# A fused transformer kernel: the bonus term, the chunk decay and the halving of tanh in the RWKV pairs are placed elsewhere

## The chip, the cores and the metric

The kernel runs on one core of a Trainium2 chip. Its time is device microseconds, the median of several runs. The engines are called PE (TensorE, the matmuls), PEld (its weight loads), DVE (VectorE), ACT (ScalarE), POOL (GpSimd) and SP (SyncE, here only for transfers).

## The reference

A first block of two layers (mixers, cross attention, convolutional feed-forward) runs over 512 tokens of width 1024 and is not touched. The second block has an RWKV-7 mixer with 8 heads of 64 channels, beside a banded attention. What matters, cut from the reference:

```python
def token_shift(p, mu):
    prev = jnp.pad(p, ((0, 0), (1, 0), (0, 0)))[:, :-1]
    return p + mu * (prev - p)

def rwkv7_step(state, inp):
    r_t, w_t, k_t, v_t, a_t, b_t = inp
    sa = jnp.einsum('bhij,bhj->bhi', state, a_t)
    state = state * w_t[:, :, None, :] + sa[..., None] * b_t[:, :, None, :] + v_t[..., None] * k_t[:, :, None, :]
    y = jnp.einsum('bhij,bhj->bhi', state, r_t)
    return state, y

def rwkv7_mix(ps, w0, w2, a0, a2, k_k, k_a, r_k, lnx_g, lnx_b):
    ...
    w_log = -jax.nn.softplus(-(w0 + jnp.tanh(wd) @ w2).astype(f32)) - 0.5
    decay = jnp.exp(-jnp.exp(w_log))
    a = jax.nn.sigmoid((a0 + ad @ a2).astype(f32))
    ...
    kk = k * k_k.astype(f32).reshape(N_RWKV_HEADS, HEAD_DIM)
    kk = kk / jnp.maximum(jnp.sqrt(jnp.sum(kk * kk, axis=-1, keepdims=True)), 1e-12)
    k = k * (1.0 + (a - 1.0) * k_a.astype(f32).reshape(N_RWKV_HEADS, HEAD_DIM))
    _, y = lax.scan(rwkv7_step, state0, (r, decay, k, v, -kk, kk * a))   # over the tokens
    ...
    bonus = jnp.sum(r * k * r_k.astype(f32), axis=-1, keepdims=True) * v
    y = y + bonus.reshape(b_, s_, D_RWKV)
    return y.astype(ps.dtype), g
```

(`y` is normalised per head between the scan and the bonus.)

## The kernel before

The second block works on transposed data: 128 channels on the partitions, 512 tokens along the free axis. Two heads make one tile, so the RWKV mixer is four pairs, `rwkv_pair(0)` to `rwkv_pair(3)`. Each pair is worked out for eight chunks of 64 tokens at once; then `rwkv_invert` inverts the 64 x 64 triangles of all pairs, through two transfers by way of DRAM, and `rwkv_chain` walks through the eight chunks, with the state of all four pairs in one tile `st`.

All through this stretch, PE is also given linear products of the second block's input projections, each a run of 24 matmuls (8 slices of K, three terms each: L304, L305 and L306) into one PSUM bank of tag "mm". They are the background: `fill(us)` hands out some microseconds' worth of them at places written into `rwkv_pair` (the table `FILL`), `need(...)` hands out as many as a pair needs to have its r, k and v. A scheduler then orders the instructions of each engine; the pair's own work has high priority, the matmuls and transposes stay in the order in which the program issues them. PSUM has 2 banks of tag "mm", 2 of "at", 1 of "pv" and 3 of "ch".

An "mm" bank of r, k or v is read by the token shift: an ACT copy `t` (L839), a DVE multiply-add over columns 1 to 511 (L841), and a DVE correction of column 0 alone (L843, 128x1). Only when all have read it can the next linear products use that bank.

The steps of a pair, in the order in which it needs them: the two lora products `pw`, `pa` (tags ch), the square of k (ACT L952), two tanh (ACT L954), each made a sigmoid by a DVE multiply-add (L955), the norm product `pk` against `ones_h`, DVE L959, the reciprocal root (L390 to L394: an ACT table load and activation, ACT square, three DVE instructions), kk (DVE L962), the new k (ACT L964, DVE L965), **the bonus** (DVE L967 makes r * r_k * k, a product `pb` against `ones_h` sums it over each head, DVE L971, ACT L972, a transfer of the result to DRAM, `yd`, by POOL's queue), the running sum of the decay's exponent (DVE scan L977) and its exponentials, the tiles `ar` (L986, L987 POOL) and `bk` (L991 DVE and L992 POOL, half of the partitions each; L988 POOL multiplies kk for it), eight transposes of v with DVE copies into `sav` (L1010 to L1015), the products of `ar` with `bk`, 32 in all, their masks (DVE L1033), a transfer of the triangles for the inversion, the decay of bk to the end of its chunk (DVE L1044, `c<-c,pc`) and its transposes, 16 products of `mk1` with `sav`, each of them for both heads, and the copy of their result to `y` (ACT L1061).

The table's `rt` is the tag of six rotating 128x512 tiles (`sg`, `av`, `q`, `u`, `kk`, `pt`), `c` the tag of bk, `rk` that of r, k and v, `xh` and `w` those of the background's operands.

## Time and profile before

| | |
|---|---|
| runs | 1797.75 us, median of 3 (1796.97 to 1798.38) |
| profiled execution | 1802.54 us, of which the span is 1800.8 us |
| mean granted clock of PE | 0.989 |
| busy | PE 98%, PEld 82%, DVE 60%, ACT 41%, POOL 25% |
| second block's pairs, inversion and chain | about 1425 to 1700 us of the span |

The rows further on come from the profiled execution. Its span is counted from the first to the last instruction; starts are microseconds from the span's begin. A row of the timeline gives start, duration, engine, line, operation and output<-inputs, and in brackets how long the engine idled ahead of it and which instruction ended that. A duration includes time in which the instruction had started and was held up. "PEclk" is the granted clock as a share of full speed.

### The profile page before, as it was taken

What the parts mean: (1) busy time and instruction counts of PE and PEld (TensorE: products, weight loads), DVE (VectorE), ACT (ScalarE), POOL (GpSimd) and SP (SyncE); (2) the same over time, 40 slices, a digit from 0 to 9 for tenths busy, and PEclk for the clock granted to TensorE, in tenths of its full rate; (3) what the DMA queues carried; (4) which work ended last, traced back from release to release, by engine and by line L of the source; (5) the groups of instructions that cost most, each with busy time, mean ns of one, the idle gap of its engine ahead of it and who ended that gap; (6) DMA issues with size and microseconds to landing.
All of it is one profiled execution on the core that took longest, in us unless ns stands there. A gap on an engine that the chain in (4) does not pass through costs nothing.

```text
span 1800.8 us, 25750 instructions
## 1 busy us (share of the span) xinstructions
PE 1761.9 (98%) x10200; PEld 1474.8 (82%) x10200; DVE 1088.5 (60%) x1649; ACT 745.3 (41%) x1231; POOL 443.7 (25%) x500
## 2 busy tenths in 40 slices
PE   8999999999999999999999999999999989999999
PEld 7889989888888888888998988888888866776667
DVE  5675756864653468544565675465455785774672
ACT  5544544532332347332354453233234543434561
POOL 0125115110100042000511543554354142210122
PEclk9999999999999999999999999999999999999999
DMA  8431312653532244432131256676663434461332
GB/s 283 155 106 48 129 36 71 206 181 115 196 99 94 74 125 130 140 94 94 50 127 36 71 193 228 245 275 227 221 226 104 137 123 179 177 199 65 136 124 92
DMA packets 67096, 252.50 MB, mean 140 GB/s; under 512 B 7840, under 2 KB 10528, under 8 KB 59296
## 3 DMA queue, kind: packets, MB, share of 16 engines
q1 hardware_dynamic: 47376, 175.92, 29.7%
q0 software_dynamic: 14768, 66.07, 10.4%
q10 hardware_dynamic: 4832, 8.88, 1.5%
q8 instruction: 80, 1.31, 0.3%
q14 instruction: 40, 0.33, 0.1%
HBM read 212.30 MB, written 38.54 MB: 139 GB/s over the span
## 4 chain that ended last, share of the span: by engine, by line
PE 82%; DVE 10%; ACT 4%; issue 2%; DMA 2%; SPq 0%; ACTq 0%; DVEq 0%
PE ch L305 11%; PE ch L304 11%; PE ch L306 11%; PE mm L304 10%; PE mm L306 10%; PE mm L305 10%; PE pv L305 4%; PE pv L304 3%; PE pv L306 3%; PE ch L907 3%; DVE x L447 1%; DVE xh L451 1%; PE at L1266 1%; DVE w L230 1%; DVE x L446 1%
## 5 line engine op out<-in xcount | busy, mean ns | idle before, releaser
L304 PE MATMUL mm<-xh,w 128*128 128x512 f32 (+1 forms) x680 | 258.2, 380 | 9.8 <-ACT w L229 6.5
L306 PE MATMUL mm<-xh,w 128*128 128x512 f32 (+1 forms) x680 | 252.6, 372 | 0.8 <-DVE w L230 0.8
L305 PE MATMUL mm<-xh,w 128*128 128x512 f32 (+1 forms) x680 | 251.5, 370 | 0.0
L229 ACT CAST w<-raw 128x1024 fp32r<-128x1024 f32 (+2 forms) x98 | 98.7, 1008 | 151.7 <-PE ch L306 62.7
L304 PEld LDWEIGHTS mm<-xh,w 128*128 128x128 f32 x680 | 130.1, 191 | 37.3 <-issue 9.6
L229 ACT CAST wx<-raw 128x1024 fp32r<-128x1024 f32 (+1 forms) x85 | 88.1, 1039 | 160.9 <-PE ch L306 68.9
L305 PE MATMUL ch<-xh,w 128*128 128x512 f32 (+1 forms) x424 | 151.5, 357 | 0.3
L304 PE MATMUL ch<-xh,w 128*128 128x512 f32 (+1 forms) x424 | 150.8, 356 | 1.0 <-ACT xh L450 1.0
L306 PE MATMUL ch<-xh,w 128*128 128x512 f32 (+1 forms) x424 | 150.5, 355 | 0.0
L306 PEld LDWEIGHTS mm<-xh,w 128*128 128x128 f32 x680 | 130.1, 191 | 24.8 <-issue 3.2
L305 PEld LDWEIGHTS mm<-xh,w 128*128 128x128 f32 x680 | 130.3, 192 | 24.4 <-issue 4.6
L230 DVE TENSOR_TENSOR w<-rawx,w 128x1024 fp32r<-128x1024 f32 (+2 forms) x85 | 116.2, 1367 | 52.6 <-ACT w L229 52.2
L230 DVE TENSOR_TENSOR w<-raw,w 128x1024 fp32r<-128x1024 f32 (+2 forms) x90 | 122.9, 1367 | 40.0 <-ACT w L229 39.4
L230 DVE TENSOR_TENSOR wx<-raw,wx 128x1024 fp32r<-128x1024 f32 (+1 forms) x85 | 117.5, 1384 | 26.5 <-ACT wx L229 26.1
L414 POOL TENSOR_TENSOR t<-x,x 128x512 f32<-128x512 f32 x6 | 8.5, 1417 | 498.3 <-DVE x L423 333.0
L229 ACT CAST w<-rawx 128x1024 fp32r<-128x1024 f32 (+2 forms) x85 | 87.3, 1027 | 100.0 <-PE mm L306 57.3
L304 PE MATMUL ch<-xh,wx 128*128 128x512 f32 (+1 forms) x288 | 100.7, 350 | 0.0
L306 PE MATMUL ch<-xh,wx 128*128 128x512 f32 (+1 forms) x288 | 100.2, 348 | 0.0
L305 PE MATMUL ch<-xh,wx 128*128 128x512 f32 (+1 forms) x288 | 100.2, 348 | 0.0
L304 PE MATMUL mm<-hd,w 128*128 128x256 f32 (+1 forms) x292 | 94.7, 325 | 0.0
L306 PE MATMUL mm<-hd,w 128*128 128x256 f32 (+1 forms) x292 | 94.7, 324 | 0.0
L305 PE MATMUL mm<-hd,w 128*128 128x256 f32 (+1 forms) x292 | 94.7, 324 | 0.0
(499 smaller groups left out, 4450.3 us busy)
## 6 DMA issues: line engine op xcount, KB each, us to landing
raw<-in_up SPq DMA_DIRECT2D x56, 512.0 KB, 3.6
sp_in_r<-vt POOLq DMA_DIRECT2D x20, 1024.0 KB, 5.2
w<-sp_in_r SPq DMA_DIRECT2D x20, 1024.0 KB, 5.0
rawx<-in_up SPq DMA_DIRECT2D x32, 512.0 KB, 3.6
kt<-in_ada POOLq DMA_DIRECT2D x24, 512.0 KB, 5.7
raw<-in_dn SPq DMA_DIRECT2D x24, 512.0 KB, 4.2
vt<-in_in_r POOLq DMA_DIRECT2D x20, 512.0 KB, 6.8
raw<-in_c_in SPq DMA_DIRECT2D x16, 512.0 KB, 3.5
```

The source lines that it names most:

```text
L229: nc.scalar.copy(hi, src)
L230: (eng or nc.vector).tensor_tensor(out=lo, in0=src, in1=f32(hi), op=ALU.subtract)
L304: mm(out, lhsT=ah, rhs=bh, start=start, stop=False)
L305: mm(out, lhsT=ah, rhs=bl, start=False, stop=False)
L306: mm(out, lhsT=al, rhs=bh, start=False, stop=stop)
L414: eng.tensor_tensor(out=sz, in0=self.x[0][:, ts] if m == 1 else sz, in1=z, op=ALU.add)
L446: (nc.vector if k in DVE_SUB else nc.gpsimd).tensor_tensor(out=x, in0=x, in1=mn, op=ALU.subtract)
L447: nc.vector.scalar_tensor_tensor(out=x, in0=x, scalar=gk, in1=rs, op0=ALU.mult, op1=ALU.mult)
L451: nc.vector.scalar_tensor_tensor(out=lo, in0=x, scalar=bk, in1=f32(hi), op0=ALU.add, op1=ALU.subtract)
L907: self.tc.keep_in_program_order(self.nc.tensor.matmul(out, **kw))
L1266: nc.tensor.matmul(ps[hs, :w], lhsT=q[hs, c * 64 : c * 64 + 64], rhs=k[hs, :w], start=True, stop=True)
```

## The change

Three edits in the second block:

- The bonus moves from the middle of a pair to its end. r * r_k * k is made behind the masks (L1039 in the new numbering); the product against `ones_h`, the multiply by v (L1061), the activation (L1062) and the transfer stand behind the pair's last products and the copy of `y`.
- The decay to the chunk's end is no longer multiplied into `bk` (L1044 goes), nor into the old state in the middle of a chunk's step; the sum of the old state and the step's products is multiplied once, behind the addition. The first step multiplies what it copied before.
- The sigmoid's `0.5 * tanh + 0.5` is an ACT activation (L958) in place of a DVE instruction.

```diff
--- before.py
+++ after.py
@@ -827,6 +827,8 @@
             nc.vector.tensor_scalar(out=t, in0=self.vec[:, s : s + n], scalar1=0.5, scalar2=None, op0=ALU.mult)
         self.qg = self.const.tile([P, 1], F32, tag="qg", name="qg")
         nc.vector.tensor_scalar(out=self.qg, in0=self.v("q_norm_g_2", 0), scalar1=0.125, scalar2=None, op0=ALU.mult)
+        self.half = self.const.tile([P, 1], F32, tag="half", name="half")
+        nc.vector.memset(self.half, 0.5)
         self.reset = self.pool.tile([P, S], BF16, tag="reset", name="reset")
         nc.vector.memset(self.reset, 1.0)
         nc.vector.memset(self.reset.rearrange("p (c t) -> p c t", c=8)[:, :, 0:1], 0.0)
@@ -942,6 +944,7 @@
         wad = self.got[16]
         self.need(self.got, (j, 4 + j, 8 + j))
         r, k, v = self.got[j], self.got[4 + j], self.got[8 + j]
+        got_v = v
         cs = slice(j * P, j * P + P)
         pa, pw = self.bank("ch"), self.bank("ch")
         self.mm(pw, lhsT=self.lora[0:64, cs], rhs=wad[0:64, :], start=True, stop=True)
@@ -952,7 +955,7 @@
         nc.scalar.activation(q, k, AF.Square, scale=self.v("k_k_2", j))
         for o, ps, b in ((sg, pw, self.hw0), (av, pa, self.ha0)):
             nc.scalar.activation(o, ps, AF.Tanh, bias=b[:, j : j + 1], scale=0.5)
-            nc.vector.tensor_scalar(out=o, in0=o, scalar1=0.5, scalar2=0.5, op0=ALU.mult, op1=ALU.add)
+            nc.scalar.activation(o, o, AF.Identity, bias=self.half, scale=0.5)
         self.fill(FILL[0])
         pk = self.bank("ch")
         self.mm(pk, lhsT=self.c("ones_h"), rhs=q, start=True, stop=True)
@@ -963,14 +966,7 @@
 
         nc.scalar.activation(u, av, AF.Identity, bias=self.ka1[:, j : j + 1], scale=self.v("k_a_2", j))
         nc.vector.tensor_tensor(out=k, in0=k, in1=u, op=ALU.mult)
-
-        nc.vector.scalar_tensor_tensor(out=u, in0=r, scalar=self.v("r_k_2", j), in1=k, op0=ALU.mult, op1=ALU.mult)
         self.fill(FILL[1])
-        pb = self.bank("ch")
-        self.mm(pb, lhsT=self.c("ones_h"), rhs=u, start=True, stop=True)
-        nc.vector.scalar_tensor_tensor(out=u, in0=pb, scalar=64.0, in1=v, op0=ALU.mult, op1=ALU.mult)
-        nc.scalar.activation(u, u, AF.Identity, bias=self.v("lnx_b_2", j))
-        nc.gpsimd.dma_start(out=self.yd[j], in_=u)
 
         e = float(np.exp(-0.5))
         c = q
@@ -1040,8 +1036,9 @@
                                     in_=m1[ob : ob + 32, hh, :, 32 * b : 32 * b + 32])
             nc.scalar.copy(sav[o : o + 32, :, o : o + 32], m1[o : o + 32, hh, :, 32:64])
 
+        nc.vector.scalar_tensor_tensor(out=u, in0=r, scalar=self.v("r_k_2", j), in1=k, op0=ALU.mult, op1=ALU.mult)
+
         bkf = bk.rearrange("p c b t -> p c (b t)")
-        nc.vector.tensor_tensor(out=bkf, in0=bkf, in1=pc.unsqueeze(2).to_broadcast([P, 8, P]), op=ALU.mult)
         bh = self.big("bh").rearrange("p (c t) -> p c t", c=8)
         for c4 in range(2):
             self.fill(FILL[4])
@@ -1059,6 +1056,11 @@
                 o, v = slice(64 * hh, 64 * hh + 64), slice(64 - 64 * hh, 128 - 64 * hh)
                 self.mm(ps[o, cc * 64 : cc * 64 + 64], lhsT=m1[v, hh, cc, :], rhs=sav[v, cc, o], start=True, stop=True)
         nc.scalar.copy(y, ps)
+        pb = self.bank("ch")
+        self.mm(pb, lhsT=self.c("ones_h"), rhs=u, start=True, stop=True)
+        nc.vector.scalar_tensor_tensor(out=u, in0=pb, scalar=64.0, in1=got_v, op0=ALU.mult, op1=ALU.mult)
+        nc.scalar.activation(u, u, AF.Identity, bias=self.v("lnx_b_2", j))
+        nc.gpsimd.dma_start(out=self.yd[j], in_=u)
         return dict(j=j, ar=ar, mk=m2, bh=bh, sav=sav, pc=pc, y=y)
 
     def rwkv_invert(self, prs):
@@ -1146,9 +1148,6 @@
                     for i, pr in enumerate(prs):
                         for o in heads:
                             self.mm(ps[o, col(i)], lhsT=st[o, i, :], rhs=pr["ar"][o, cc, 1, :], start=i == 0, stop=False)
-                    if cc < 7:
-                        nc.vector.tensor_tensor(out=st, in0=st, in1=pc4[:, :, cc : cc + 1].to_broadcast([P, 4, 64]),
-                                                op=ALU.mult)
                     yield
                 for i in range(4):
                     for o in heads:
@@ -1165,10 +1164,12 @@
                         self.mm(ps[o, col(i)], lhsT=sav4[:, i, cc, o], rhs=pr["mk"][:, hh, cc, :], start=False, stop=i == 3)
                 if cc < 7:
                     sn = self.t("st", [P, 256], F32, 2).rearrange("p (i t) -> p i t", i=4)
-                    if cc == 0:
-                        nc.vector.tensor_copy(sn, four(ps[:, 256:]))
-                    else:
-                        nc.vector.tensor_tensor(out=sn, in0=st, in1=four(ps[:, 256:]), op=ALU.add)
+                    got = four(ps[:, 256:])
+                    if cc:
+                        nc.vector.tensor_tensor(out=sn, in0=st, in1=got, op=ALU.add)
+                        got = sn
+                    nc.vector.tensor_tensor(out=sn, in0=got, in1=pc4[:, :, cc : cc + 1].to_broadcast([P, 4, 64]),
+                                            op=ALU.mult)
                     st = sn
                 nc.scalar.copy(rs, four(ps[:, :256]))
                 yield
```

The new line numbers are two or three higher than the old ones down to the bonus's old place (the token shift's L839, L841 and L843 become L841, L843 and L845; the tanh's L954 becomes L957), and three or four lower behind it (bk's L991, L992 and L988 become L987, L988 and L984, the masks' L1033 becomes L1029).

How the order of the engines' instructions moves, at three places. First DVE in pair 1, between the norm's multiplies and the products of `ar` and `bk`; `mm_12312` is the bank of the last-but-one linear output before PE's next two, `sav` the transposed v, `c_1618` or `c_1617` is bk. Before:

```order
L841 SCALAR_TENSOR_TENSOR rk_12371<-mm_12312,mu_12054,t_1620_12372 128x511
L393 TENSOR_SCALAR rt_12304<-rt_12304 128x512
L977 SCALAR_TENSOR_TENSOR rt_12303<-reset,rt_12301 128x512
L394 TENSOR_TENSOR rt_12322<-rt_12322,rt_12304 128x512
L843 TENSOR_SCALAR rk_12371<-mm_12312,mu_12054 128x1
L962 SCALAR_TENSOR_TENSOR rt_12322<-rk_12177,vec,rt_12322 128x512
L994 COPY pc_1563_12076<-rt_12354 128x8
L965 TENSOR_TENSOR rk_12177<-rk_12177,rt_12304 128x512
L986 SCALAR_TENSOR_TENSOR ar_12358<-rt_12322,rt_12301 128x8x64
L967 SCALAR_TENSOR_TENSOR rt_12304<-rk_12097,vec,rk_12177 128x512
L841 SCALAR_TENSOR_TENSOR rk_12420<-mm_12378,mu_12054,t_1627_12421 128x511
L991 TENSOR_TENSOR c_1618_12359<-rt_12322,rt_12303 64x8x64
```

And of the changed kernel, in which L843 of the same bank (`rk_12366<-mm_12313`) stands one row ahead of this piece:

```order
L965 SCALAR_TENSOR_TENSOR rt_12323<-rk_12173,vec,rt_12323 128x512
L1006 COPY sav_1562_12077<-ch_12380 64x4x64
L990 COPY pc_1563_12078<-rt_12349 128x8
L1008 COPY sav_1562_12077<-ch_12380 64x3x64
L1009 COPY sav_1562_12077<-ch_12380 64x64
L968 TENSOR_TENSOR rk_12173<-rk_12173,rt_12305 128x512
L982 SCALAR_TENSOR_TENSOR ar_12353<-rt_12323,rt_12302 128x8x64
L1006 COPY sav_1562_12077<-ch_12398 64x4x64
L1011 COPY sav_1562_12077<-ch_12398 64x4x64
L987 TENSOR_TENSOR c_1617_12354<-rt_12323,rt_12304 64x8x64 x2
L1039 SCALAR_TENSOR_TENSOR rt_12305<-rk_12099,vec,rk_12173 128x512
L845 TENSOR_SCALAR rk_12366<-mm_12313,mu_12054 128x1
```

The 128x1 correction of that bank (L843 before, L845 now) has moved from behind the third multiply of the norm to behind both halves of bk and the moved r * r_k * k (L967 before, L1039 now); the copies of v stand ahead of the new k (L965 before, L968 now), where they were behind bk.

Second, PE in the same pair: linear products (`mm`), the bonus product (`ch_12347<-rt_12304,cst`) and the transposes of v (`ch<-cst,rk`). Before:

```order
L305 MATMUL mm_12427<-w_12457,xh_11203 128x512
L306 MATMUL mm_12427<-w_12457,xh_11203 128x512
L304 MATMUL mm_12427<-w_12457,xh_11204 128x512
L907 MATMUL ch_12347<-rt_12304,cst 128x512
L910 MATMUL ch_12385<-cst,rk_12226 64x128
L907 MATMUL ch_12385<-cst,rk_12226 64x64
L910 MATMUL ch_12385<-cst,rk_12226 128x128 x3
L910 MATMUL ch_12403<-cst,rk_12226 128x128 x4
L305 MATMUL mm_12427<-w_12457,xh_11204 128x512
```

Now, at the end of the linear products that lie ahead of the products of `ar` and `bk`; the two banks `mm_12422` and `mm_12423` are the ones given back by the two token shifts of the piece of DVE above:

```order
L304 MATMUL mm_12422<-w_12424,xh_11202 128x512
L304 MATMUL mm_12423<-w_12424,xh_11201 128x512
L305 MATMUL mm_12423<-w_12424,xh_11201 128x512
L306 MATMUL mm_12423<-w_12424,xh_11201 128x512
L305 MATMUL mm_12422<-w_12424,xh_11202 128x512
L306 MATMUL mm_12422<-w_12424,xh_11202 128x512
L304 MATMUL mm_12423<-w_12424,xh_11202 128x512
L305 MATMUL mm_12423<-w_12424,xh_11202 128x512
L306 MATMUL mm_12423<-w_12424,xh_11202 128x512
L909 MATMUL at_12439<-ar_12353,c_1617_12354 128x128
L909 MATMUL ch_12438<-ar_12353,c_1617_12354 128x128
```

The bonus product is gone from this place, the transposes of v stand 21 to 30 linear products ahead of the products of `ar` and `bk`, and the linear products into the next two banks stand last in between.

Third, ACT where pair 2 begins, from the copy of `y` on. Before:

```order
L1061 COPY y_1561_12074<-ch_12559 128x512
L839 ACTIVATE t_1647_12581<-mm_12537,vec 128x512
L952 ACTIVATE rt_12591<-rk_12580,vec 128x512
L954 ACTIVATE rt_12589<-ch_12586,hw_12058 128x512
L954 ACTIVATE rt_12590<-ch_12585,ha_12059 128x512
L390 ACT_TABLE_LOAD
L390 ACTIVATE rt_12610<-rt_12591,eps 128x512
```

Now:

```order
L1058 COPY y_1561_12076<-ch_12554 128x512
L841 ACTIVATE t_1647_12581<-mm_12532,vec 128x512
L1062 ACTIVATE rt_12305<-rt_12305,vec 128x512
L955 ACTIVATE rt_12591<-rk_12580,vec 128x512
L957 ACTIVATE rt_12589<-ch_12586,hw_12058 128x512
L957 ACTIVATE rt_12590<-ch_12585,ha_12059 128x512
L958 ACTIVATE rt_12589<-rt_12589,half 128x512
L958 ACTIVATE rt_12590<-rt_12590,half 128x512
L390 ACT_TABLE_LOAD
L390 ACTIVATE rt_12610<-rt_12591,eps 128x512
```

The activation of the bonus of pair 1 (L1062) stands ahead of pair 2's square and tanh, and both halvings (L958) stand between the tanh and the table load for the reciprocal root.

## Rows read from the trace of the kernel before

**Rows 1.** The page, busy time of each engine
```profile
PE 1761.9 (98%) x10200; PEld 1474.8 (82%) x10200; DVE 1088.5 (60%) x1649; ACT 745.3 (41%) x1231; POOL 443.7 (25%) x500
```

**Rows 2.** Waits from 1430 to 1630 us (total, times, longest)
```profile
PE ch L907 <- DVE rt L967: 10.1, 4, 2.9
```

**Rows 3.** Timeline of PE, at five places
```profile
1454.78 1.10 PE L907 MATMUL ch<-rt,cst 128*128 128x512 f32 x2 [2.13 <-DVE rt L967]
...
1455.71 0.27 PE L910 MATMUL ch<-cst,rk 128*64 128x128 f32 x1
...
1475.51 0.39 PE L304 MATMUL mm<-w,xh 128*128 128x512 f32 x1
...
1560.01 1.10 PE L910 MATMUL ch<-cst,c 128*128 128x128 f32 x8
...
1612.26 0.47 PE L304 MATMUL mm<-xh,w 128*128 128x512 f32 x1 [3.27 <-issue]
```

**Rows 4.** Timeline of DVE at the inversion
```profile
1610.11 1.29 DVE L1100 STREAM_TRANSPOSE rt<-c 32x512 f32<-32x512 f32 x2 [4.65 <-DMA c<-dt]
...
1611.96 0.19 DVE L843 TENSOR_SCALAR t<-mm,mu 128x1 f32<-128x1 f32 x1
```

**Rows 5.** Table of stretches: length, busy time (instructions) by engine, clock, DMA
```profile
1466.50:1477.90 11.40, 11.40 (x50) 8.96 (x48) 9.05 (x14) 8.52 (x12) 3.77 (x3) 1.00 0.37 119
...
1456.40:1459.80 3.40, 3.40 (x26) 3.07 (x26) 3.28 (x8) 0.72 (x1) 0.60 (x1) 0.50 0.00 0
...
1480.30:1487.10 6.80, 6.29 (x17) 4.18 (x18) 5.49 (x11) 0.72 (x1) 2.20 (x2) 0.50 0.10 39
...
1613.40:1616.80 3.40, 3.40 (x10) 2.66 (x9) 2.34 (x5) 0.63 (x1) 0.57 (x1) 0.51 0.85 346
```

**Rows 6.** Timeline of DVE in pairs 0, 2 and 3
```profile
1454.56 2.45 DVE L991 TENSOR_TENSOR c<-rt,rt 64x512 f32<-64x512 f32 x2
...
1457.76 0.43 DVE L1010 COPY sav<-ch 64x256 f32<-64x256 f32 x1
...
1461.48 1.21 DVE L1044 TENSOR_TENSOR c<-c,pc 128x1024 f32<-128x1024 f32 x1
...
1521.32 2.45 DVE L991 TENSOR_TENSOR c<-rt,rt 64x512 f32<-64x512 f32 x2
...
1551.01 2.45 DVE L991 TENSOR_TENSOR c<-rt,rt 64x512 f32<-64x512 f32 x2
```

**Rows 7.** Timeline of DVE in pair 1
```profile
1466.73 0.43 DVE L955 TENSOR_SCALAR rt<-rt 128x512 f32<-128x512 f32 x1 [2.59 <-ACT rt L954]
...
1473.71 0.21 DVE L843 TENSOR_SCALAR rk<-mm,mu 128x1 f32<-128x1 f32 x1
...
1477.80 2.96 DVE L967 SCALAR_TENSOR_TENSOR rt<-rk,vec,rk 128x512 f32<-128x512 f32 x1
...
1482.93 0.69 DVE L971 SCALAR_TENSOR_TENSOR rt<-ch,rk 128x512 f32<-128x512 f32 x1 [0.49 <-PE ch L907]
...
1483.65 0.69 DVE L991 TENSOR_TENSOR c<-rt,rt 64x512 f32<-64x512 f32 x1
```

**Rows 8.** Timeline of POOL in pair 1
```profile
1478.96 1.25 POOL L988 TENSOR_TENSOR rt<-rt,rt 128x512 f32<-128x512 f32 x1
...
1480.29 1.60 POOL L992 TENSOR_TENSOR c<-rk,rt 64x512 f32<-64x512 f32 x1
```

**Rows 9.** Timeline of ACT where pairs 1, 2 and 3 begin
```profile
1464.96 0.59 ACT L1061 COPY y<-ch 128x512 f32<-128x512 f32 x1
...
1466.01 0.69 ACT L954 ACTIVATE rt<-ch,hw 128x512 f32<-128x512 f32 x1 [0.46 <-PE ch L907]
...
1504.30 0.59 ACT L1061 COPY y<-ch 128x512 f32<-128x512 f32 x1 [5.26 <-PE ch L907]
...
1536.14 0.58 ACT L1061 COPY y<-ch 128x512 f32<-128x512 f32 x1 [0.45 <-PE ch L907]
```

**Rows 10.** The instructions of L1171 (duration in ns, min/median/max; starts)
```profile
L1171 DVE TENSOR_TENSOR st<-st,ch x6: 420/420/422, 1646.0 to 1696.6; 128x256 f32<-128x256 f32 x6
```

## The prediction

> **What bounds the kernel now.** I first read the page: PE is busy 98% of the span, 1761.9 of 1800.8 us [rows 1]. So time comes or goes in two ways only: PE gets more or fewer products, or a place appears or goes where PE waits. The change leaves PE's list of products as it is (the same products, only in another order), so the whole question is PE's waits in the stretch from about 1445 to 1700 us.
>
> Next the list of waits for that stretch. PE has one large entry: four waits for L967, 10.1 us in sum [rows 2]. Each is the bonus product, which PE meets before the scaled r*k is ready; the first is the 2.13 us before 1454.78 [rows 3]. A fifth wait, 3.27 us before 1612.26, carries no releaser's name [rows 3]; VectorE shows it. There a transpose stood 4.65 us for a DMA, and behind it, in order, stood the two token-shift instructions whose second (L843, 1611.96) gives a PSUM bank of tag "mm" back [rows 4].
>
> Then the table of stretches. PE ran at the granted clock 0.50, the 1.2 GHz level, for some time behind each of these waits: 3.4 us from 1456.4, 6.8 us from 1480.3, two more such stretches of 3.4 us behind the last two pairs' waits, 3.4 us from 1613.4 [rows 5]. Half of that time is lost, since the same products run at twice the rate at the upper level: 8.5 us behind the four waits and 1.7 behind the fifth. The first begins 3.75 us after its wait began (1456.4 against 1454.78-2.13).
>
> **What the change takes away.** The four waits for L967 go, 10.1 us: the bonus product now stands behind a pair's last products, and its input was made long before. L1044, 1.21 us a pair [rows 6], goes from VectorE, where it stood between the masks and the transposes of bk. PE's waits name no such transpose; in the last pair they start at 1560.01 right behind other products [rows 3]. So I cost L1044 at nothing: PE's linear products cover it, and if that cover were gone it would be worth its 1.21 us a pair (in rival D).
>
> **What L967 is worth to the chain.** It reads 2.96 us in the rows, but ends at 1480.76, and GpSimd's L988, whose output both VectorE halves of bk (L991) read, ends only at 1480.21; GpSimd's second L992 ends at 1481.89 [rows 7, 8]. The instruction is long because it sits beside GpSimd. Without it VectorE stands before L991 for almost as long. So between 0 and 0.56 us a pair; I take 0.2, and only in pairs 0 to 2, since in pair 3 it still stands ahead of bk under its new line.
> The Trainium skill, "SBUF — State Buffer", Who interferes with whom, says the same of such a pair: a VectorE instruction with two SBUF inputs and a GpSimd one share a port as an exclusive lock. By it the gain is near 0; by the row's face value it would be 2.4 us a pair (rival A).
>
> **What it puts on the path.** In the new order PE meets the bk products (L909) directly, with no bonus product ahead. What must be ready is bk, and its chain (tanh, rsqrt, kk, k, bk) gets longer:
> - Bonus activation (L1062) ahead of the next pair's tanh on ScalarE. Pair 1: the y copy starts at 1464.96 and the tanh at 1466.01 [rows 9]. Now the bonus product, 0.93 (1454.78 to 1455.71 [rows 3]), runs until 1465.9, a VectorE multiply of 0.7 until 1466.7, and the activation, 0.7 as the tanh beside it, until 1467.45: +1.45, in pairs 1 and 3. In pair 2 ScalarE waits for the next k anyway, whose last three products now stand behind the bonus product: +0.93. Pair 0 has no predecessor.
> - Two halvings on ScalarE ahead of the table load and rsqrt: 2 x 0.67 = +1.35 (+1.04 in pair 0, where a part lies beside other work). On VectorE they lay in gaps: L955 at 1466.73 followed 2.59 us of idling for ScalarE's tanh [rows 7]. Bounds 0 and 1.4 a pair.
> - The copies of the transposed v now stand in the middle of the chain: 0.43 for the largest [rows 6], three of them; part lies beside a stretch that GpSimd blocks. +0.7, bounds 0 and 3 x 0.43 = 1.3.
> - In pair 1 the wait for the bonus product and L971 ahead of the second L991 (0.49+0.69 = 1.2 us [rows 7]) go, and some 0.3 of token shift; in pair 2 some 0.2 of it.
>
> bk was ready at 1457.01 in pair 0 (1454.56+2.45 [rows 6]), 1484.34 in pair 1 [rows 7], 1523.77 and 1553.46 in pairs 2 and 3 [rows 6]. Counted from the y copy of the pair before [rows 9], that is 19.4, 19.5 and 17.3 us. New: pair 0 1457.0+1.04+0.7-0.2 = 1458.5; pair 1 19.4+1.45+1.35+0.7-0.2-1.5 = 21.2; pair 2 19.5+0.93+1.35+0.7-0.2-0.2 = 22.1; pair 3 17.3+1.45+1.35+0.7 = 20.8.
>
> **The bank.** The one-column correction of the token shift, the last reader of an "mm" bank, stood just behind the norm's multiplies and gave its bank back by 1473.9 in pair 1 (1473.71+0.21 [rows 7]); PE took it without waiting at 1475.51 [rows 3]. Now (L845) it stands behind both halves of bk and the moved L1039, so the bank comes free 0.6+0.2 after bk: 22.0 in pair 1, and 22.9 in pair 2, where it is the same. PE needs that bank 12 products before it comes to bk. In pair 3 no such products stand between.
>
> **When PE arrives.** Linear products pass at 0.24 us each (48 to 50 in 11.40 us [rows 5]); bonus, tanh-input pair and norm product take 0.93 each, eight transposes of v 1.1 (as those at 1560.01 [rows 3]). Pair 0: free at 1452.65, three products fewer (-0.7), transposes first: 1453.1. Pair 1: 2.8+47 x 0.24+1.1 = 15.2 after the y copy. Pair 2: 2.8+51 x 0.24+1.1 = 16.1. Pair 3: 2.8+50 x 0.24+1.1+0.9 for an attention product = 16.8.
>
> **The sum.** Waits: pair 0 1458.5-1453.1 = 5.4; pair 1 22.0-15.2 = 6.8; pair 2 22.9-16.1 = 6.8; pair 3 20.8-16.8 = 4.0, and there 1.7 more before the sav products, since three attention multiplies now stand ahead of the masks on VectorE. Together 24.7 for 10.1: +14.6. Before the inversion's products PE now brings 2.5 us of work that stood earlier (three linear products, the last bonus product and an attention product), and the DMA starts 0.3 earlier: the wait of 3.27 shrinks to 0.4, -2.9. Clock: the slow stretch behind that wait goes (-1.7); behind the others, a stretch that begins 3 to 4 us after the wait's start now lies partly inside a wait of 5 to 7 us and costs less (-1.3, bounds -3.5 and 0): -3.0. In the chain of eight chunks the new multiply stands behind the addition, 0.42 us each [rows 10]; PE has linear products between, so +0.2 (bounds 0 and 0.5). In all +14.6-2.9-3.0+0.2 = +8.9.
>
> The profiled execution took 1802.54 us (1800.8 and 1.74 around it), 4.8 above the runs' median of 1797.75. The profile after should give 1811.4, the runs **1806.5**. Its own range is 1801 to 1811: halvings half covered (-2.8), the bank not binding in one of two pairs (-4), no return from the clock (+1.3), GpSimd stretched further by the new neighbours (+0.7 a pair).
>
> **Rivals.**
> A, not slower: L967's full length comes off. For: 2.96 us in the row. Against: L988 ends at 1480.21 [rows 8]. It decides from where GpSimd's L988 starts some 2 us earlier than before, counted from the y copy. 2.2 us a pair more than taken, in four pairs: 8.9-8.8, **1797.8**, no change.
> B: the bank doesn't bind, as the one-column correction is fast enough or PE's products come later. Then only bk counts: pair 1 21.2-(15.2+2.9) = 3.1, pair 2 22.1-19.0 = 3.1, 7.4 less: +1.5, **1799.3**, no change.
> C: the chunk chain pays for the serial multiply, 7 x 0.45 = 3.1 on top: **1809.6**. Against: the linear products between the steps.
> D, faster: the change does what its parts suggest, and work leaves VectorE on the path: 0.43 x 2+1.21+0.56 = 2.6 a pair, 10.5 in four, **1787.2**. Against: VectorE's idling ahead of L955 [rows 7]. The Trainium skill, "Perfetto Trace Analysis", Optimizing Scalar/DVE Operations, says that offloading some work to Scalar may make sense if DVE is saturated; by it the halvings would bring up to 8 x 0.43 = 3.4 us, but at the 60% of [rows 1] DVE is not saturated.
>
> **Chances.** The forecast 0.60, A 0.11, B 0.14, C 0.06, D 0.09. A measurement of this kernel can tell 0.2%, 3.6 us, from no change. Faster: D and part of A, 0.13. Same: B, most of A and the lower tail of the forecast, 0.24. Slower: 0.63. The range that leaves out D and the tails: 1795.5 to 1811.
>
> **What would show it.** PE's waits at the bonus product are gone. In pair 0 a wait of some 5 us before the bk products, released by L987 or GpSimd's L988; in pairs 1 and 2 waits of 6 to 7 us at an "mm" product, released by VectorE's L845; in pair 3 some 4 and 1.7; the one at the inversion under 1 us; L1039 short, some 0.65. No wait in the chain. It is wrong if bk is ready at about the old distance from the y copy (the halvings or the copies lay in gaps), or if L845 runs before bk.

## The result, and the profile after

The changed kernel took 1811.84 us, median of 4 runs (1808.15 to 1815.83), beside 1797.36 us for the kernel before (median of 4). The ratio is 1.0086, 95% interval 1.0064 to 1.0108: 14.5 us slower. Measured again beside other kernels it was 1.0076 (1.0058 to 1.0094). The forecast was slower, by 8.9 us, at 1806.5 in a range of 1795.5 to 1811; the time lies 0.8 us above the range. The profiled execution took 1815.83 us, so its span of 1814.0 us is 4.0 above the median's, and 13.2 us longer than the span before [rows 1].

The page of the changed kernel, the span and the engines' busy time:

```profile
span 1814.0 us, 25741 instructions
...
PE 1764.8 (97%) x10200; PEld 1478.8 (82%) x10200; DVE 1069.0 (59%) x1638; ACT 750.3 (41%) x1239; POOL 447.8 (25%) x500
```

VectorE lost 19.5 us of work and PE gained 2.9 us of busy time on the same products; the other 10.3 us are PE's gaps. The list of waits from 1430 to 1645 us (total, times, longest):

```profile
PE mm L304 <- issue: 15.7, 3, 6.2
...
PE at L909 <- DVE c L987: 7.8, 2, 4.5
...
PE at L1242 <- ACT t L1238: 0.8, 1, 0.8
```

The four waits for L967 [rows 2] are gone. In their place stand two for bk and two at linear products; the third wait at a linear product is the inversion's. The timeline of PE says where:

```profile
1456.73 0.34 PE L909 MATMUL at<-ar,c 64*128 64x128 f32 x1 [4.48 <-DVE c L987]
...
1483.61 0.77 PE L304 MATMUL mm<-w,xh 128*128 128x512 f32 x1 [5.65 <-issue]
...
1528.72 0.77 PE L304 MATMUL mm<-xh,w 128*128 128x512 f32 x1 [6.23 <-issue]
...
1560.77 0.55 PE L909 MATMUL at<-ar,c 64*128 64x128 f32 x1 [3.33 <-DVE c L987]
...
1621.71 0.76 PE L304 MATMUL mm<-xh,w 128*128 128x512 f32 x1 [3.83 <-issue]
```

Pairs 0 to 3 wait 4.48, 5.65, 6.23 and 3.33 us, 19.7 in sum, for 10.1 before: +9.6. The wait at the inversion did not shrink, 3.83 for 3.27 [rows 3]. The second and the third are the bank: in VectorE's timeline of pair 1 the correction that frees it, L845, ends at 1483.51 (1483.30 and 0.21), 0.1 us before PE goes on.

```profile
1478.33 0.42 DVE L1011 COPY sav<-ch 64x256 f32<-64x256 f32 x1
1480.24 2.36 DVE L987 TENSOR_TENSOR c<-rt,rt 64x512 f32<-64x512 f32 x2 [1.49 <-POOL rt L984]
1482.63 0.75 DVE L1039 SCALAR_TENSOR_TENSOR rt<-rk,vec,rk 128x512 f32<-128x512 f32 x1
1483.30 0.21 DVE L845 TENSOR_SCALAR rk<-mm,mu 128x1 f32<-128x1 f32 x1
```

L1039 is the old L967 in its new place: 0.75 us in pairs 0 to 2, where it read 2.96 beside GpSimd [rows 7]; in pair 3, where it still stands ahead of bk, it reads 3.02. VectorE idled for 1.49 us ahead of bk for GpSimd's kk*av, and what was left of the two token shifts on which the banks hang, 1.1 us of work, stood behind it.

GpSimd's part of the chain did not move either. The new k in the kernel before:

```profile
1476.59 0.68 DVE L965 TENSOR_TENSOR rk<-rk,rt 128x512 f32<-128x512 f32 x1
```

And in the changed kernel, with GpSimd's instructions behind it:

```profile
1476.59 0.67 DVE L968 TENSOR_TENSOR rk<-rk,rt 128x512 f32<-128x512 f32 x1
...
1477.40 1.59 POOL L988 TENSOR_TENSOR c<-rk,rt 64x512 f32<-64x512 f32 x1 [1.26 <-DVE rk L968]
1478.95 1.26 POOL L984 TENSOR_TENSOR rt<-rt,rt 128x512 f32<-128x512 f32 x1
```

GpSimd's kk*av starts 1.69 us after the new k is complete, as before (1478.96 [rows 8]): moving L967 did not bring it forward.

What the waits cost beyond themselves shows in the table of stretches of the changed kernel (columns as in [rows 5]):

```profile
1412.70:1416.10 3.40, 2.92 (x7) 2.36 (x8) 3.40 (x8) 3.40 (x9) 0.00 (x0) 0.50 0.17 70
...
1560.80:1566.40 5.60, 5.60 (x41) 5.34 (x41) 5.40 (x13) 0.76 (x2) 0.79 (x2) 0.51 0.05 19
1621.70:1627.80 6.10, 6.09 (x15) 4.77 (x16) 3.49 (x6) 1.78 (x3) 1.95 (x7) 0.50 0.60 218
1638.00:1648.20 10.20, 10.20 (x64) 5.61 (x58) 2.55 (x13) 4.37 (x13) 0.54 (x1) 0.50 0.08 29
```

And two stretches of the kernel before:

```profile
1412.10:1418.90 6.80, 6.25 (x15) 4.99 (x16) 3.87 (x8) 4.49 (x11) 0.00 (x0) 0.50 0.22 77
1627.10:1633.90 6.80, 6.80 (x69) 4.74 (x63) 1.19 (x3) 2.93 (x6) 0.00 (x0) 0.50 0.01 2
```

PE worked at the lower level for 6.1 us behind the inversion's wait, where it was 3.4 before [rows 5], and for 10.2 us at the chain's begin, where it was 6.8: half of the difference, 3 us, is lost time more. Behind the pairs' waits the working time at the lower level is about as long as before, 16.6 for 16.3 us: the stretches behind pairs 2 and 3 are twice as long as before (6.8 us for 3.4), and lie partly inside the waits. One stretch goes the other way: behind a wait of 2.7 us that both kernels have ahead of the first pair, PE worked 2.9 us at the lower level for 6.25 before, 1.7 us less lost. These lengths are not the same in every execution: a second profile of the changed kernel (changed_again, span 1810.8 us) has the same 19.7 us of waits, no slow stretch behind that wait and one of 13.7 us at the chain's begin, of which PE worked 11.3.

### The profile page after: what moved, and what is told of

It is laid out like the page before. It is cut to its first block, busy times and chain, and to the rows that moved or that the text cites. A ratio compares the mean times of both kernels' runs of the same rounds, so it can differ in the third digit from the quotient of the medians.

```text
span 1814.0 us, 25741 instructions
## 1 busy us (share of the span) xinstructions
PE 1764.8 (97%) x10200; PEld 1478.8 (82%) x10200; DVE 1069.0 (59%) x1638; ACT 750.3 (41%) x1239; POOL 447.8 (25%) x500
## 3 DMA queue, kind: packets, MB, share of 16 engines
q0 software_dynamic: 14768, 66.07, 10.2%
## 4 chain that ended last, share of the span: by engine, by line
PE 82%; DVE 9%; ACT 4%; issue 3%; DMA 2%; POOL 0%; SPq 0%; ACTq 0%; DVEq 0%; POOLq 0%
PE ch L304 11%; PE ch L305 11%; PE ch L306 11%; PE mm L304 10%; PE mm L306 10%; PE mm L305 10%; PE pv L305 4%; PE pv L304 4%; PE pv L306 4%; PE ch L909 2%; PE at L1267 1%; DVE x L447 1%; DVE xh L451 1%; DVE w L230 1%; DVE x L446 1%
## 5 line engine op out<-in xcount | busy, mean ns | idle before, releaser
L304 PE MATMUL mm<-xh,w 128*128 128x512 f32 (+1 forms) x680 | 262.0, 385 | 16.1 <-issue 10.1
L304 PEld LDWEIGHTS mm<-xh,w 128*128 128x128 f32 x680 | 131.6, 194 | 46.3 <-issue 19.5
L305 PEld LDWEIGHTS mm<-xh,w 128*128 128x128 f32 x680 | 131.8, 194 | 24.3 <-issue 4.9
L306 PEld LDWEIGHTS mm<-xh,w 128*128 128x128 f32 x680 | 131.4, 193 | 24.0 <-issue 2.3
L230 DVE TENSOR_TENSOR w<-rawx,w 128x1024 fp32r<-128x1024 f32 (+2 forms) x85 | 108.9, 1282 | 54.5 <-ACT w L229 54.1
L230 DVE TENSOR_TENSOR wx<-raw,wx 128x1024 fp32r<-128x1024 f32 (+1 forms) x85 | 122.3, 1441 | 28.2 <-ACT wx L229 26.4
```

The source lines that it names most:

```text
L230: (eng or nc.vector).tensor_tensor(out=lo, in0=src, in1=f32(hi), op=ALU.subtract)
L304: mm(out, lhsT=ah, rhs=bh, start=start, stop=False)
L305: mm(out, lhsT=ah, rhs=bl, start=False, stop=False)
L306: mm(out, lhsT=al, rhs=bh, start=False, stop=stop)
```

## The experiments

Ratios are to the kernel before, run beside it on the same chip; the changed kernel stands at 1.0086 and 1.0076. "Waits" is the sum of PE's four waits in the pairs, from each profile.

| kernel | ratio (95%) | waits, us |
|---|---|---|
| before | 1 | 10.1 |
| changed | 1.0086 (1.0064 to 1.0108) | 19.7 |
| bonus_only | 1.0070 (1.0054 to 1.0085) | 18.6 |
| half_only | 1.0054 (1.0039 to 1.0069) | 14.5 |
| decay_only | 1.0014 (1.0003 to 1.0026) | 9.2 |
| after_yd_late | 1.0117 (1.0101 to 1.0134) | 19.7 |
| after_half_dve | 1.0094 (1.0077 to 1.0111) | 16.8 |
| after_act_shift | 1.0047 (1.0028 to 1.0066) | 15.1 |
| after_av | 1.0102 (1.0085 to 1.0120) | 19.4 |
| before_av | 1.0023 (1.0006 to 1.0040) | 12.4 |
| before_dve | 0.9942 (0.9922 to 0.9962) | 1.1 |
| after_dve | 1.0048 (1.0032 to 1.0064) | 14.3 |
| act_shift_dve_half | 0.9944 (0.9927 to 0.9961) | 3.0 |
| before_dve_act | 0.9940 (0.9919 to 0.9962) | 2.4 |
| changed_again | 1.0076 (1.0058 to 1.0094) | 19.7 |
| half_dve_again | 1.0066 (1.0048 to 1.0084) | 16.8 |
| act_shift_dve | 0.9961 (0.9941 to 0.9981) | 5.9 |

### The three edits, each alone

**bonus_only**: the bonus's five instructions at the pair's end, L1044 and the VectorE sigmoid kept.

```diff
-        nc.vector.scalar_tensor_tensor(out=u, in0=r, scalar=self.v("r_k_2", j), in1=k, op0=ALU.mult, op1=ALU.mult)
         self.fill(FILL[1])
-        pb = self.bank("ch")
...
         nc.scalar.copy(y, ps)
+        pb = self.bank("ch")
...
+        nc.gpsimd.dma_start(out=self.yd[j], in_=u)
```

> Only the bonus is moved to the pair's end; decay of bk and sigmoid stay as before. Theory (the move takes four waits of 10.1 us in sum away, but puts PE before a bk that is late, and puts the bonus activation ahead of the next tanh and the last pair's transfer ahead of the inversion's load): the four waits come back as 13 to 15 us at the bk products or at the linear products ahead of them, the inversion's load starts some 7 us later than before, +5 to +9 us over the kernel before, about 1804. Rival (the loss of the whole change comes from the halvings on ScalarE): no change, within 3 us of the kernel before.

Measured: 1.0070, some 12.6 us slower by the ratio and 10.9 by the medians, more than the 5 to 9 expected. The waits are 3.90, 6.02, 5.11 and 3.52 us, 18.6 in sum, the middle two at linear products, as in the changed kernel; more than the 13 to 15 expected. The rival, that the loss comes from the halvings, is refuted: nearly all of the changed kernel's waits come with the move alone. The inversion's load is issued at 1567.20; counted from the last common wait of PE ahead of the pairs (it ends at 1407.94 here, at 1412.65 before) that is 5.9 us later than before.

**half_only**:

```diff
-            nc.vector.tensor_scalar(out=o, in0=o, scalar1=0.5, scalar2=0.5, op0=ALU.mult, op1=ALU.add)
+            nc.scalar.activation(o, o, AF.Identity, bias=self.half, scale=0.5)
```

> Only the sigmoid's halving is an activation on ScalarE; all else as before. Theory (both halvings stand between the tanh and the table load of the reciprocal root, so r*r_k*k and bk are ready some 1.0 to 1.35 us later in each pair): PE's four waits for r*r_k*k grow from 10.1 to 14 to 15.5 us, +4 to +6 us. Rival (work leaves VectorE, 0.43 us twice a pair): -3.4 us. Second rival (the halvings lie in ScalarE's gaps): within 1 us.

Measured: 1.0054, 9.7 us slower by the ratio and 7.2 by the medians, more than expected. ScalarE's timeline where pair 1 begins, and the waits:

```profile
1464.25 0.69 ACT L956 ACTIVATE rt<-ch,hw 128x512 f32<-128x512 f32 x1 [0.46 <-PE ch L909]
1464.97 0.72 ACT L957 ACTIVATE rt<-rt,half 128x512 f32<-128x512 f32 x1
1465.60 0.67 ACT L956 ACTIVATE rt<-ch,ha 128x512 f32<-128x512 f32 x1
1466.30 0.72 ACT L957 ACTIVATE rt<-rt,half 128x512 f32<-128x512 f32 x1
1467.04 1.28 ACT L390 ACT_TABLE_LOAD   x1
...
PE ch L909 <- DVE rt L969: 14.5, 4, 4.1
```

In the kernel before the load stands here:

```profile
1467.29 1.28 ACT L390 ACT_TABLE_LOAD   x1
```

From the first tanh to the table load 2.79 us pass; before, 1.28 (1466.01 [rows 9] to 1467.29): the load is 1.5 us later. The same four waits as before grow from 10.1 to 14.5 us; bk is ready 0.7, 1.2, 1.2 and 1.5 us later, counted from its pair's begin. So this edit alone, which takes 0.86 us a pair off VectorE, makes the kernel slower, and the sign of rival D is refuted. The rest of the loss, 5.3 us by the ratio and 2.8 by the medians, is not in these waits. The two profiled executions differ by 3.9 us (spans of 1804.7 and 1800.8), which is no more than the waits. The profile shows PE at the lower clock for 13.6 us at the chain's begin, for 6.8 before, but decay_only has a stretch of 13.7 us there too, so that this is not shown to be the rest.

**decay_only**: L1044 out, the new state multiplied behind its addition (the lines of the diff above).

> Only the decay is moved from bk and the old state to the new state. Theory (L1044 was covered by linear products, and the added multiply of the chain by others): within 1.5 us of the kernel before, PE's waits unchanged. Rival (L1044 stood on the path): -4.8 us (4 x 1.21). Second rival (the chain pays for the multiply): +3 us.

Measured: 1.0014, 2.5 us slower, with an interval from 0.5 to 4.7. This lies between the theory's 1.5 and the second rival's 3 and decides nothing between them; that L1044 stood on the path is refuted. PE's four waits for L967 are 9.2 us, with two short ones that are new (0.65 us at a linear product for L843, 0.46 ahead of the sav products), so L1044 was worth nothing there. In the chain PE waits once, 0.91 us.

### The inversion

**after_yd_late**: the changed kernel, the last pair's transfer behind the inversion's load on GpSimd's queue.

```diff
+        if j < 3:
             nc.gpsimd.dma_start(out=self.yd[j], in_=u)
...
+        self.tc.keep_in_program_order(
             nc.gpsimd.dma_start(out=nb, in_=self.dn.rearrange("b n s t -> (b n) (s t)"))
+        )
+        self.tc.keep_in_program_order(nc.gpsimd.dma_start(out=self.yd[3], in_=prs[3]["u"]))
```

> The changed kernel, with the last pair's bonus transfer issued behind the inversion's load on GpSimd's queue in place of ahead of it. Theory (that transfer holds the load back): the load is issued some 3 to 4 us earlier than in the changed kernel, counted from the last pair's products, PE's wait of 3.83 us at the inversion shrinks below 1 us and the slow clock behind it goes, 4 to 6 us off the changed kernel's time, +8 to +10 over the kernel before. Rival (the load waits for the triangles' transfers, whatever stands ahead): within 1 us of the changed kernel, +13 to +15 over the kernel before.

Measured: 1.0117, not faster than the changed kernel. GpSimd's queue in the changed kernel:

```profile
1565.61 2.34 POOL L1035 DMA_DIRECT2D dn<-mk  x4 [6.23 <-DVE mk L1029]
1573.56 0.60 POOL L1063 DMA_DIRECT2D yd<-rt  x1 [5.61 <-issue]
1574.29 0.56 POOL L1070 DMA_DIRECT2D c<-dn  x1
```

And with the transfer behind the load:

```profile
1560.04 2.35 POOL L1035 DMA_DIRECT2D dn<-mk  x4 [6.22 <-DVE mk L1029]
1566.64 0.60 POOL L1071 DMA_DIRECT2D c<-dn  x1 [4.25 <-PE mm L306]
1567.23 0.56 POOL L1072 DMA_DIRECT2D yd<-rt  x1
```

From the triangles' first transfer to the load 8.7 us become 6.6: the bonus's transfer did stand in the way, for 2.1 us. But PE's wait at the inversion grew from 3.83 to 5.78. The table of transfers shows where: on the way of the inverse to DRAM (KB, us from issue to landing), first in the changed kernel:

```profile
dt<-c POOLq DMA_DIRECT2D x1, 512.0 KB, 4.0
```

And in after_yd_late, with what SP's queue issued just ahead of it:

```profile
dt<-c POOLq DMA_DIRECT2D x1, 512.0 KB, 6.9
...
1599.53 0.32 SPq L282 DMA_DIRECT2D w<-sp_in_r  x1
```

Here it was issued at 1599.89, 0.4 us behind a weight transfer of 1 MB; in the changed kernel at 1608.28, 2.3 us behind such a one. The 2.1 us won at the load were lost at the store.

### What holds bk and the bank

**after_half_dve** and, beside the changed kernel on one chip, **half_dve_again** (the same kernel): the changed kernel with the VectorE sigmoid back.

> The changed kernel with the sigmoid's halving back on VectorE. Theory (the halvings lengthen the chain to bk by 0.9 to 1.35 us a pair): PE's waits ahead of bk fall from 19.7 us to 15 to 16, 4 to 5 us off the changed kernel, +9 to +11 over the kernel before. Rival (the chain's end is set by GpSimd and the bank, the halvings lie in gaps): within 1.5 us of the changed kernel, +13 to +16.

> The changed kernel with the halving on VectorE, beside the changed kernel on one chip. Theory (the halvings' 2.9 us of waits ahead of bk are real and partly given back later): 1 to 4 us under the changed kernel. Rival (with bk and the bank late for other reasons the halvings are worth nothing in the time): within 1 us of it.

> The changed kernel once more, beside the two others of this call on one chip. All theories: +12 to +18 us over the kernel before.

Measured: 1.0094 on one chip, 1.0066 beside the changed kernel's 1.0076 on another, 1.6 us less by the medians, with intervals that overlap. The waits fall by 2.9 us in both profiles. So in the changed kernel the halvings cost 2.9 us of waits, and the time does not tell their price from nothing; it is less than the 4 to 5 us expected.

**after_act_shift**: ScalarE makes both factors of the token shift, so that the bank is free without VectorE, which only adds.

```diff
-        nc.vector.scalar_tensor_tensor(out=out[:, 1:], in0=ps[:, 1:], scalar=mu1, in1=t[:, : S - 1],
-                                       op0=ALU.mult, op1=ALU.add)
-        nc.vector.tensor_scalar(out=out[:, 0:1], in0=ps[:, 0:1], scalar1=mu1, scalar2=None, op0=ALU.mult)
+        nc.scalar.activation(out, ps, AF.Copy, scale=mu1)
+        nc.vector.tensor_tensor(out=out[:, 1:], in0=out[:, 1:], in1=t[:, : S - 1], op=ALU.add)
```

> The changed kernel, with the token shift's second factor made on ScalarE too, so that ScalarE alone frees the mm bank and VectorE only adds. Theory (in pairs 1 and 2 PE waits for the bank, not for bk): the waits of 5.65 and 6.23 us at linear products go, 12 linear products pass, and a wait of 2 to 3.5 us at the products of ar and bk stands in their place; 4 to 6 us off the changed kernel, +8 to +11 over the kernel before. Rival (bk is as late and the clock or ScalarE's 0.7 us more a tile take it back): within 2 us of the changed kernel.

Measured: 1.0047, 5 to 7 us off the changed kernel's 1.0076 and 1.0086. Its waits:

```profile
PE at L908 <- DVE c L986: 15.1, 4, 4.0
```

No linear product waits any more; all four waits are for bk. In pair 1 it is 4.02 for 5.65 us, in pair 2 3.82 for 6.23. The bank is shown as the cause of the two longest waits. They shrank by less than expected, as bk itself is later here (23.2 us after pair 2's begin for 21.5, ScalarE has more to do). The wait at the inversion's linear product (3.83 us) is gone too: that bank stood behind VectorE's transpose, as before [rows 4], and ScalarE frees it. PE waits 1.76 us for a later link of the inversion in its place.

**after_av** and **before_av**: GpSimd writes kk*av over av and not over kk, so that it can run ahead of the new k.

```diff
-        nc.gpsimd.tensor_tensor(out=kk, in0=kk, in1=av, op=ALU.mult)
+        nc.gpsimd.tensor_tensor(out=av, in0=kk, in1=av, op=ALU.mult)
```

> The changed kernel, with kk*av written over av in place of over kk, so that GpSimd makes it ahead of the two halves of k's part of bk. Theory (bk waits for GpSimd's kk*av, which stood behind the new k): bk is ready 1.3 to 1.8 us earlier in each pair, the four waits fall from 19.7 to 13 to 15 us, 5 to 7 us off the changed kernel, +8 to +10 over the kernel before. Rival (the sum of GpSimd's and VectorE's exclusive instructions sets bk, in whatever order): within 1.5 us of the changed kernel.

> The kernel before, with kk*av written over av, so that GpSimd makes it ahead of the two halves of k's part of bk. Theory (L967 is long because GpSimd's second and third instruction hold it up): L967 and bk end 1.2 to 1.5 us earlier, PE's four waits fall from 10.1 to 4 to 6 us, 4 to 6 us faster than the kernel before. Rival (L967 ends where GpSimd's next instruction lets it, in either order): within 2 us of the kernel before.

Measured: 1.0102 and 1.0023; no gain in the first, and the second is slower than the kernel before by about 4 us. GpSimd and VectorE of before_av in pair 1:

```profile
1473.60 1.78 POOL L988 TENSOR_TENSOR rt<-rt,rt 128x512 f32<-128x512 f32 x1
1475.35 3.38 POOL L992 TENSOR_TENSOR c<-rk,rt 64x512 f32<-64x512 f32 x2
...
1474.19 1.74 DVE L986 SCALAR_TENSOR_TENSOR ar<-rt,rt 128x512 f32<-128x512 f32 x1
1475.85 1.74 DVE L967 SCALAR_TENSOR_TENSOR rt<-rk,vec,rk 128x512 f32<-128x512 f32 x1
1477.52 2.45 DVE L991 TENSOR_TENSOR c<-rt,rt 64x512 f32<-64x512 f32 x2
```

L988 runs early, but now L986 is the long one (1.74 for 0.68), and L967 still takes 1.74. The order does not matter: the two engines take turns, and each of GpSimd's instructions costs VectorE about 1.0 to 1.1 us wherever it stands (L986 1.74 for 0.68, L967 1.74 for 0.73). The rival held. That the four waits grew to 12.4 us is not explained by this: the new k itself came 0.8 to 1.1 us later in pairs 1 to 3, and no run shows why.

**before_dve** and **after_dve**: kk*av and k's two halves of bk on VectorE.

```diff
-        nc.gpsimd.tensor_tensor(out=kk, in0=kk, in1=av, op=ALU.mult)
+        nc.vector.tensor_tensor(out=kk, in0=kk, in1=av, op=ALU.mult)
...
-            nc.gpsimd.tensor_tensor(out=bk[hs, :, 1 - hh, :], in0=ch(k)[hs], in1=ch(c)[hs], op=ALU.mult)
+            nc.vector.tensor_tensor(out=bk[hs, :, 1 - hh, :], in0=ch(k)[hs], in1=ch(c)[hs], op=ALU.mult)
```

> The kernel before, with kk*av and k's two halves of bk on VectorE in place of GpSimd. Theory (from the new k to bk, VectorE and GpSimd take turns, and GpSimd takes 1.25 to 1.6 us for what VectorE does in some 0.65): r*r_k*k is ready 2 to 2.4 us earlier after k and bk 1.5 to 2.5 us earlier; PE's four waits fall from 10.1 us to 1 to 4, 4 to 9 us faster than the kernel before. Rival (both are bound by k itself or VectorE's queue): within 2 us of the kernel before.

> The changed kernel, with kk*av and k's two halves of bk on VectorE. Theory (the same turns set bk here): bk 1.2 to 2 us earlier after k, the waits of 19.7 us fall to 12 to 15, 4 to 7 us off the changed kernel, +7 to +11 over the kernel before. Rival (the inversion's collision with weight transfers and the slow clock take it back): within 2 us of the changed kernel.

Measured: 0.9942 and 1.0048. The first is 9.9 us faster than the kernel before (1788.33 for 1798.18). VectorE in its pair 1, and PE's waits:

```profile
1472.28 0.68 DVE L965 TENSOR_TENSOR rk<-rk,rt 128x512 f32<-128x512 f32 x1
1472.88 0.67 DVE L986 SCALAR_TENSOR_TENSOR ar<-rt,rt 128x512 f32<-128x512 f32 x1
1473.49 0.73 DVE L967 SCALAR_TENSOR_TENSOR rt<-rk,vec,rk 128x512 f32<-128x512 f32 x1
1474.15 0.68 DVE L988 TENSOR_TENSOR rt<-rt,rt 128x512 f32<-128x512 f32 x1
...
1477.34 0.69 DVE L992 TENSOR_TENSOR c<-rk,rt 64x512 f32<-64x512 f32 x1
...
PE ch L907 <- DVE rt L967: 0.9, 2, 0.5
```

L967 takes 0.73 us, bk is complete 5.1 us after k (1478.03 against 1472.96; 7.1 before) though VectorE makes all of it, and the waits of 10.1 us are down to 1.1. No stretch of the pairs runs at the lower clock any more, where PE worked 16.3 us at it before; in the second block the first begins at 1602.4, at the inversion, and is longer than before (15.8 us of work for 10.2 there and at the chain's begin). So about half of what the pairs gain is the clock's. In the changed kernel the same edit brings 5 to 7 us: the bank still holds PE for 5.03 and 5.64 us in pairs 1 and 2, while pairs 0 and 3 fall to 3.07 and 0.59.

**act_shift_dve_half**, **act_shift_dve** and **before_dve_act** put these together: the changed kernel with ScalarE's bank and VectorE's bk, with the halvings on VectorE and on ScalarE, and the kernel before with ScalarE's bank and VectorE's bk.

> The changed kernel with three things mended: bank freed by ScalarE alone, kk*av and k's halves of bk on VectorE, halvings back on VectorE. Theory (bank, turns and halvings are the three causes of the late bk, and add up): the four waits fall from 19.7 us to 6 to 10, the time comes to within 4 us of the kernel before. Rival (the move of the bonus costs by itself, through the later tanh and the later inversion): +5 or more over the kernel before.

> The changed kernel with the bank freed by ScalarE and kk*av and k's halves of bk on VectorE, but the halvings left on ScalarE. Theory (once bank and turns are mended, bk's chain is what PE waits for, and the halvings lengthen it by 0.9 to 1.35 us a pair): 3 to 6 us over the same kernel with halvings on VectorE, which ran at 0.9944 of the kernel before, so 0.996 to 0.998. Rival (PE's waits of 0.4 to 1 us a pair are no longer set by that chain): within 1 us, 0.994 to 0.995.

> The kernel before with kk*av and k's halves of bk on VectorE, and the bank freed by ScalarE alone. Theory (before, the bank was free in time, so that this adds nothing to the first): within 2 us of the same kernel without the ScalarE bank. Rival (the bank of the later token shift bound there too, or stands behind the longer VectorE queue): 2 to 5 us faster than that.

Measured: 0.9944, 0.9961 and 0.9940. With all three mended the change is some 24 us faster than as it was made (0.9944 against 1.0076 to 1.0086), 10 us under the kernel before where within 4 was expected, and level with before_dve: the waits for bk are 3.0 us, less than the 6 to 10 expected (with the halvings on ScalarE 5.9; that is 3 us in the time, intervals overlapping). The move of the bonus, and that of the decay, cost nothing that shows in the time then. Nor do they bring anything over before_dve, whose waits for the bonus product had gone in the same way. before_dve_act is the same as before_dve, so the bank did not bind there; in the kernel before itself no linear product of the pairs waits.

```profile
PE at L906 <- DVE c L984: 3.0, 4, 1.1
PE at L1239 <- ACT t L1235: 2.6, 1, 2.6
```

(act_shift_dve_half, list of waits; the second is at an attention product, while the inversion runs.)

## Why the prediction came out as it did

**Right: the direction, and the mechanism of the pairs' waits.** The wait did not go, it moved to bk and to the bank, at the instructions that were named. PE's arrival was right: 15.2 and 16.3 us after the y copy at which pairs 1 and 2 begin (forecast 15.2 and 16.1), 16.7 in pair 3 (16.8). So was the tanh, later by 1.36, 0.86 and 1.36 us (1.45, 0.93, 1.45), from the bonus activation ahead of it:

```profile
1462.75 0.58 ACT L1058 COPY y<-ch 128x512 f32<-128x512 f32 x1 [0.18 <-PE ch L909]
...
1464.52 0.72 ACT L1062 ACTIVATE rt<-rt,vec 128x512 f32<-128x512 f32 x1 [1.19 <-DVE rt L1061]
1465.15 0.67 ACT L957 ACTIVATE rt<-ch,hw 128x512 f32<-128x512 f32 x1
```

**The term of the waits was too large.** Forecast +14.6, measured +9.6. In pairs 0 to 3 the waits are 4.5, 5.7, 6.2 and 3.3 for 5.4, 6.8, 6.8 and 4.0. bk came 19.9, 21.5 and 19.9 us after the y copy at which pairs 1 to 3 begin, for 21.2, 22.1 and 20.8. From the tanh to the new k, halvings and copies of v together added 0.84, 1.72 and 1.18 us in these pairs, for the 2.05 put down; half_only, with the halvings alone, adds 1.18 to 1.51. From the new k to bk L967's leaving gave 0.54 us in pairs 0 and 2, for 0.2. The copies of v cost nothing in the chain (+0.7 was put down): they ran where VectorE had been held up anyway, as at the multiply that makes kk, which fell from 1.66 us (L962 before) to 1.13 (L965 now). And the 1.7 us ahead of the sav products did not show as a wait: PE was at the lower clock then, worked 5.6 us at it, and came to the sav products at 1566.61, behind the last mask (1566.31).

**The terms of what is given back failed, and took the time past the range.** Forecast -2.9 at the inversion and -3.0 by the clock; measured +0.6, and by the clock +1.5 at the places that were named and +1.7 at the chain's begin, which was not. At the inversion the step "the DMA starts 0.3 earlier" was wrong: the load came 6.5 us behind the end of the last pair's products, where it had been 3.8. The last bonus's transfer stood ahead of it on GpSimd's queue, as after_yd_late shows for 2.1 us of it. PE brought some 3 us more work there, as forecast, but VectorE's transpose was later by as much, and an attention multiply of 0.7 us ran between it and the token shift. By the clock, the stretch behind the inversion's wait did not go but doubled, for the wait had not gone. The step "a stretch that begins 3 to 4 us after the wait's start" was misread: in the kernel before, the stretches of pairs 1 and 2 began 2.4 and 2.3 us after it (1480.3 for 1477.9, 1521.3 for 1519.0). The longer waits did hide part of the lower clock, but the stretches of pairs 2 and 3 became twice as long, so that nothing was given back. Two waits not forecast, 0.82 at an attention product of the inversion and 0.71 in the chain, come on top. Less the 1.7 us of the stretch ahead of the pairs, that makes 9.6+0.6+3.2+1.5-1.7 = 13.2, for 12.7 between the two profiles from the end of the wait ahead of the pairs on (1412.65 of 1800.8, 1413.18 of 1814.0); the last 0.5 is not placed, and another 0.5 between the spans lies ahead of that wait.

That the total missed by only some 5 us is luck: the waits were put 5.0 us too high and the rest about 9 too low. And the forecast's own sum, 1797.75+8.9, is 1806.65, not 1806.5.

**The rivals.** A is refuted: its sign, GpSimd's kk*av starting earlier after the y copy, did not come (16.2 us in pair 1, for 14.0). And not for the reason of one place: L967's length is GpSimd's share of the turns, and as long as GpSimd's instructions stayed, moving L967 freed 0.5 us a pair and reordering nothing (before_av, after_av); with them gone, L967 and bk both came early. B, that the bank does not bind, is refuted by after_act_shift; in the kernel before it holds (before_dve_act). C is not settled by the time: decay_only cost 0.5 to 4.7 us. The profiles put it at about 1 us, above the 0.2 put down and below C's 3.1: in each of the eleven profiles with the decay's edit PE waits once in the chain, 0.7 to 1.9 us, and in none of the six others. The changed kernel's:

```profile
1690.85 0.66 PE L1297 MATMUL at<-cst,c 128*128 128x128 f32 x4 [0.71 <-DVE sm L1270]
```

D is refuted for the halving by half_only, for L1044 by decay_only, and for the work taken off VectorE altogether by before_dve, which puts three instructions a pair onto VectorE and is faster.

The Trainium skill, "Perfetto Trace Analysis", Optimizing Scalar/DVE Operations, advises moving work to Scalar if DVE is saturated, and says that moving between DVE and GPSIMD might not help because of the shared port. The first condition was not given here, and the move cost time (1.0054); the second half agrees with the turns in these traces, and the gain came from moving work the other way.

**Left open.** Where half_only loses the 3 to 5 us that its waits don't hold, and how much of the halvings' price stays in the time of the changed kernel; why GpSimd's queue took 2.5 us from the end of the last bonus activation (1571.01) to the transfer's issue (1573.56).

## What to carry to other kernels

Before a wait is moved, ask what PE meets next in its order and when that is ready: here the wait for the bonus product had covered a bk that was late too, and with it gone the next link of the same chain was waited for longer. A last, tiny reader (0.2 us, 128x1) that falls behind a long chain holds a whole PSUM bank and everything planned into it. And an instruction that reads four times its own length (2.96 us for 0.73) beside another engine is paying for that engine: taking the other engine's three instructions over was worth 10 us, where moving, halving and sparing VectorE's own work was worth nothing or less.

## What the runs showed of the hardware

VectorE's instructions with two SBUF inputs and GpSimd's elementwise ones took turns at every place seen: L967 took 2.96 us beside two of GpSimd's and 0.73 without them. The Trainium skill, "SBUF — State Buffer", Who interferes with whom, tells of this as contention for a shared port pair, which is an exclusive lock. The trace agrees: L986 read 1.74 us beside L988 in before_av and 0.67 in before_dve, where GpSimd no longer has that work. It adds that GpSimd's turn (1.25 to 1.6 us) is about twice VectorE's for the same work (0.65). Copies from PSUM were not held: L1011 took 0.42 us at 1478.33, inside GpSimd's L988 (1477.40 to 1478.99).

The inverse's store of 512 KB from GpSimd's queue landed the later, the closer it was issued behind a weight transfer of 1 MB on SP's queue: in 3.2 us where that had been issued 3.1 us before (half_only), 3.3 at 2.7 (before), 4.0 at 2.3 (changed), 5.8 at 1.0 (act_shift_dve_half), 6.9 at 0.4 (after_yd_late) and 7.0 at 0.15 (before_dve); the other profiles fit in between, and where the weight transfer was issued 0.2 us behind the store (after_av), it took 6.8. When the two meet is set by how fast the work ahead of either ran, so a gain ahead of the inversion can cost 3.7 us there (7.0 in before_dve for 3.3 before).
